# Planned order made binding: 21 stores and 64 loads of a 4096³ matmul with gelu wait for semaphores

## The chip, the cores and the metric

The kernel runs on one core of one Trainium2 chip. The metric is the device time in microseconds (us) of one execution; each kernel is run several times and the median is given. The core has five instruction streams that run beside each other: TensorE (PE, with its weight loads shown apart as PEld), VectorE (DVE), ScalarE (ACT), GpSimd (POOL) and SyncE (SP). In this kernel POOL and SP issue the transfers: POOL all loads, SP all stores.

## The reference

```python
def setup_inputs():
    m, k, n = 4096, 4096, 4096
    return {"a": np.random.randn(m, k).astype(np.float32),
            "b": np.random.randn(k, n).astype(np.float32)}

def reference(a, b):
    x = np.matmul(a, b)
    return 0.5 * x * (1 + np.tanh(np.sqrt(2 / np.pi) * (x + 0.044715 * x**3)))
```

One 4096×4096×4096 product and a gelu in its tanh form on every element; inputs and output are float32.

## The kernel before

**Products.** A and B are each cut into 2×2 quarters, named "11", "12", "21" and "22", and the product is formed with seven products P1 to P7 of sums and differences of quarters, in float16 with float32 sums (a Strassen scheme). The output is made in 16 groups: four row blocks `mb` of A times four column blocks `nb` of B. One group is a 512×512 block in each of the four output quarters. Group 0 (`first_group`) computes part of its work plainly and so can start before the sums exist; groups 1 to 3 use the seven products; groups 4 to 15 run in pairs (`late_pair`), in which some products are split a second time.

**Data.** A cell is a tile of 128×2048 float16 (512 KB); cells are named `bR`, `aD`, `aT` and `stage` after the pool they lie in. Raw rows of A and B come from DRAM through POOL (`stage<-in_a_dram`, `bR<-in_b_dram`), which turns float32 into float16 on the way. DVE transposes A (L752) and forms the sums and differences (L1039), TensorE multiplies (L822 in group 0 to 3, L2068 in the pairs). Ready sums of B are kept: SP stores them as units to DRAM (`k_unit<-bR`, `k_unit<-aD`, `k_unit<-stage`, from `store_unit`), and POOL fetches them in later groups (`bR<-k_unit`). SP also writes the output (`out_dram<-y`). All transfers are issued in one helper, so that all have the line L913.

**The squares.** Beside the product the kernel sums squares of A and B on ACT (L1437, L1459, L1504) to learn whether float16 sums are safe for these inputs; if they are not, a plain path runs. In two pairs `weigh_again` loads rows of A a second time for that, eight times four transfers of `bR<-in_a_dram`.

**What sets the order.** The program is recorded as a list of operations. `Plan.add` (L424) notes for each its engine, its duration by a table of costs, and which earlier operations it depends on, through the cells that it reads and writes. `Plan.schedule` simulates the engines with these costs, a table `AFTER` moves some operations by hand, and `Plan.emit` (L601) writes the operations out in the order of their planned starts. On the chip each engine takes its own instructions in that order. The waits between engines come from the framework, which sees the tiles that an instruction reads and writes.

**Gates.** Some transfers are recorded with `after=`: an earlier operation behind which they are planned although they share no data with it. It takes part in the simulated schedule and so in the order of the instructions, but the framework knows nothing of it, and the engine does not wait. One single pair of operations (`HOLD`, 1645 behind 1568) has had a real wait added. The transfers with gates are these:

- In `first_group`, `gate = load_a_("12", 1)[-1:]` (L2456) is a load of the second half of A's quarter "12", of the raw rows `stage<-in_a_dram`. Behind it are planned the units P7, lower half (L2460), and P5, upper half (L2471): two transfers each, the first four stores that SP issues.
- Later in `first_group`, `send(3, ...)` and `send(9, ...)` hold back twelve output blocks behind loads for group 1. `keep_t("P4", t1, ...)` (L2524) stores two transfers behind the last load of group 1's quarter "12" of B, and P5, lower half, and P6, upper half (L2525 and L2526) four behind the last load of quarter "22".
- In the pairs, the 32 transfers of `weigh_again` (L1453) and the 16 of `cast_unit` (L1693 and L2164, `k_unit<-in_b_dram`) stand behind the product operation nine back (`CAST_BACK`), and 16 transfers of `turn_quad` stand behind a fetch of product P1's units.

**Lanes.** Every transfer adds to one of eight semaphores of its queue when it has landed, in turn (`DMASW0` to `DMASW7` for POOL's, `DMAHW0` to `DMAHW7` for SP's). A wait on such a semaphore's value is a wait for one transfer's landing.

Of the kernel before, what the change touches and what calls it, by code (L numbers as in the profile page):

```python
# [80 lines left out]
def modes_of(**kw):  # L81
# [14 lines left out]
HOLD = {  # L96
    1645: 1568,
}
# [314 lines left out]


class Op:
    __slots__ = ("n", "eng", "dur", "fn", "deps", "succ", "key", "left", "ready", "need", "front", "start", "end", "size", "weight", "every", "frees")


class Plan:
# [4 lines left out]
    def add(self, eng, dur, fn, r=(), w=(), size=0, batch=None, after=(), slack=18.0, weight=1.0, every=None, lead=0.0):  # L424
        o = Op()
        o.every = dur if every is None else every
        o.weight, o.frees = weight, []
        o.n, o.eng, o.dur, o.fn, o.size = len(self.ops), eng, dur, fn, size
        deps = set(after)
        r, w = self.halves(r), self.halves(w)  # L430
        for tok in r:
            st = self.state.setdefault(tok, [[], [], None, ()])
            deps.update(st[0])
            st[1].append(o)
        for tok in w:
            st = self.state.setdefault(tok, [[], [], None, ()])
            if batch is not None and st[2] == batch and not [x for x in st[1] if x is not o]:
                deps.update(st[3])
                st[0].append(o)
                continue  # L440
            st[3] = set(st[0]) | {x for x in st[1] if x is not o}
            deps.update(st[3])
            st[0], st[1], st[2] = [o], [], batch
        deps.discard(o)
        o.deps, o.succ, o.key = deps, [], self.now + (slack if eng != "PE" else 0.0)
        for d in deps:
            d.succ.append(o)
        o.need = self.now + (max(slack, SLACK2) if eng != "PE" else 0.0)
        o.key, o.need = (x - EARLIER.get(o.n, 0.0) - lead for x in (o.key, o.need))
        o.left, o.ready = len(deps), 0.0  # L450
        self.ops.append(o)
        if eng == "PE":
            self.now += dur
        return o
# [145 lines left out]
    def emit(self):  # L600
        self.schedule()  # L601
        self.schedule(self.moved_order())
        done = {}
        for o in sorted(self.ops, key=lambda o: (o.start, o.n)):
            o.fn()
            done[o.n] = self.tc.nc.cur_bb.bb.instructions[-1]
            if o.n in HOLD:
                self.tc.add_manual_dep(
                    done[o.n], done[HOLD[o.n]].name,
                    mybir.DependencyInfo(mybir.DependencyClass.Sync, mybir.DependencyReason.DATA),  # L610
                    reason="later",
                )
# [2007 lines left out]
```

## Time and profile before

| | before |
|---|---|
| runs, us | 1467.91, 1457.4, 1468.47 (median 1467.91) |
| profiled execution, us | 1462.97 |
| its span, first to last instruction, us | 1461.3 |
| mean granted TensorE clock | 0.994 |
| busy: PE, DVE, ACT, POOL | 1424.8, 1225.1, 684.4, 506.6 us |
| moved by DMA | 389.36 MB, mean 266 GB/s |
| of it POOL's queue (q0, software) | 255.91 MB, 74.8% of 16 engines' span |
| of it SP's queue (q1, hardware) | 132.15 MB, 24.1% |

How to read it: a row of a timeline gives start, duration, engine, line, operation, `out<-in`, shapes and count, and in brackets the idle time of the engine just before and what ended it. The releaser in the brackets is inferred from semaphore events; where the engine it names had long been done, the wait was for another thing, often a transfer. A row of the waits gives the total idle time in us, how often, and the longest. A row of the table by windows gives the window, its length, the busy time of PE, PEld, DVE, ACT and POOL (with counts), the granted clock, the DMA share and GB/s. The DMA share is the sum of the time that packets took over that of 16 engines; it can be over 1 where packets of two queues overlap on an engine. "To landing" is the time from the issue of a transfer to its landing.

### The profile page before, as it was taken

What the parts mean: (1) busy time and instruction counts of PE and PEld (TensorE: products, weight loads), DVE (VectorE), ACT (ScalarE), POOL (GpSimd) and SP (SyncE); (2) the same over time, 40 slices, a digit from 0 to 9 for tenths busy, and PEclk for the clock granted to TensorE, in tenths of its full rate; (3) what the DMA queues carried; (4) which work ended last, traced back from release to release, by engine and by line L of the source; (5) the groups of instructions that cost most, each with busy time, mean ns of one, the idle gap of its engine ahead of it and who ended that gap; (6) DMA issues with size and microseconds to landing.
All of it is one profiled execution on the core that took longest, in us unless ns stands there. A gap on an engine that the chain in (4) does not pass through costs nothing.

```text
span 1461.3 us, 19125 instructions
## 1 busy us (share of the span) xinstructions
PE 1424.8 (98%) x6707; PEld 656.6 (45%) x6707; DVE 1225.1 (84%) x1319; ACT 684.4 (47%) x1376; POOL 506.6 (35%) x924
## 2 busy tenths in 40 slices
PE   8979999999999999999999999999999999999998
PEld 3434455465444444444444444444444444444443
DVE  2786797997878999978997989878998998867877
ACT  3505555439867322443645524353453734432133
POOL 7554236054125142324333352432323242231220
PEclk9989999999999999999999999999999999999999
DMA  9999999999999998989989999999898998895764
GB/s 173 211 208 263 301 278 227 372 240 262 325 288 227 314 231 212 329 279 263 296 315 290 305 198 296 304 256 308 250 337 241 308 238 262 264 295 213 267 230 182
DMA packets 216375, 389.36 MB, mean 266 GB/s; under 512 B 21456, under 2 KB 128464, under 8 KB 216272
## 3 DMA queue, kind: packets, MB, share of 16 engines
q0 software_dynamic: 159104, 255.91, 74.8%
q1 hardware_dynamic: 57168, 132.15, 24.1%
q8 instruction: 55, 0.90, 0.2%
q14 instruction: 48, 0.39, 0.1%
HBM read 356.52 MB, written 134.22 MB: 336 GB/s over the span
## 4 chain that ended last, share of the span: by engine, by line
PE 58%; DMA 14%; DVE 4%; issue 3%; POOL 1%; ACT 0%; SPq 0%; DVEq 0%; POOLq 0%; ACTq 0%
PE acc L2068 57%; DMA bR<-in_b_dram 5%; DMA bR<-in_a_dram 3%; DMA bR<-k_unit 3%; DVE bR L1039 2%; DMA stage<-k_unit 1%; PE acc L822 1%; POOL bR L913 1%; DMA k_unit<-bR 1%; DMA out_dram<-y 1%; DVE y L1397 1%; PE acc L1120 1%; DMA stage<-in_a_dram 1%; DVE y L1509 0%; DMA stage<-in_b_dram 0%
## 5 line engine op out<-in xcount | busy, mean ns | idle before, releaser
L2068 PE MATMUL acc<-bR 128*128 128x512 f16 x1344 | 300.2, 380 | 3.1 <-DVE bR L1039 2.9
L2068 PE MATMUL acc<-bR,aT 128*128 128x512 f16 x1280 | 284.2, 379 | 5.9 <-DVE bR L1039 5.0
L2068 PEld LDWEIGHTS <-bR 128*128 128x128 f16 x1824 | 178.5, 98 | 221.9 <-issue 5.9
L2068 PEld LDWEIGHTS <-aT 128*128 128x128 f16 x1664 | 162.6, 98 | 203.9 <-DMA bR<-in_b_dram 2.8
L913 POOL DMA_DIRECT2D bR<-in_b_dram x336 | 182.2, 545 | 188.1 <-DMA bR<-in_b_dram 31.4
L913 POOL DMA_DIRECT2D bR<-k_unit x210 | 114.0, 546 | 333.2 <-PE acc L2068 199.6
L1039 DVE TENSOR_TENSOR bR<-bR 128x4096 f16<-128x4096 f16 (+1 forms) x107 | 194.8, 1828 | 24.7 <-PE acc L2068 9.1
L2080 ACT COPY acc<-acc 128x512 f32<-128x512 f32 x168 | 95.9, 575 | 252.9 <-PE acc L2068 211.5
L1397 DVE TENSOR_TENSOR y<-acc,y 128x512 f32<-128x512 f32 x269 | 175.9, 685 | 24.4 <-PE acc L2068 21.9
L2068 PE MATMUL acc<-bR,aD 128*128 128x512 f16 x752 | 167.4, 379 | 1.4 <-DVE aD L1039 0.9
L2068 PEld LDWEIGHTS <-aD 128*128 128x128 f16 x1024 | 100.1, 98 | 122.8 <-DVE aD L1039 1.4
L1371 ACT ACTIVATE y<-y 128x512 f32<-128x512 f32 x174 | 105.6, 626 | 91.5 <-DVE y L1397 91.5
L822 PE MATMUL acc<-bR,aT 128*128 128x512 f16 x544 | 120.4, 379 | 2.1 <-DMA bR<-in_b_dram 1.0
L822 PEld LDWEIGHTS <-aT 128*128 128x128 f16 x768 | 75.0, 98 | 91.8 <-issue 3.0
L1504 ACT ACTIVATE y<-bR 128x1024 bf16<-128x1024 f16 x86 | 88.5, 1052 | 56.4 <-DVE y L1509 52.4
L2068 PE MATMUL acc<-stage,bR 128*128 128x512 f16 x480 | 108.0, 379 | 0.9 <-DVE bR L1039 0.9
L2077 ACT COPY y<-acc 128x512 f32<-128x512 f32 x114 | 65.3, 586 | 81.5 <-PE acc L2068 70.1
L822 PEld LDWEIGHTS <-aD 128*128 128x128 f16 x608 | 60.2, 99 | 87.5 <-DVE aD L1039 9.4
L913 POOL DMA_DIRECT2D bR<-in_a_dram x108 | 63.2, 590 | 95.7 <-ACT y L1437 46.4
L1509 DVE TENSOR_TENSOR y<-y 128x1024 bf16<-128x1024 bf16 x102 | 69.8, 686 | 23.1 <-ACT y L1504 21.6
L1402 DVE TENSOR_TENSOR acc<-acc,y 128x512 f32<-128x512 f32 x115 | 76.7, 693 | 13.8 <-ACT y L2077 13.7
L2068 PE MATMUL acc<-stage,aT 128*128 128x512 f16 x384 | 86.8, 379 | 0.4 <-DMA stage<-k_unit 0.4
(126 smaller groups left out, 1821.9 us busy)
## 6 DMA issues: line engine op xcount, KB each, us to landing
bR<-k_unit POOLq DMA_DIRECT2D x210, 512.0 KB, 7.5
out_dram<-y SPq DMA_DIRECT2D x194, 256.0 KB, 6.5
bR<-in_b_dram POOLq DMA_DIRECT2D x344, 128.0 KB, 6.4
k_unit<-bR SPq DMA_DIRECT2D x80, 512.0 KB, 6.9
stage<-k_unit POOLq DMA_DIRECT2D x74, 512.0 KB, 7.1
bR<-in_a_dram POOLq DMA_DIRECT2D x108, 256.0 KB, 8.6
k_unit<-stage SPq DMA_DIRECT2D x28, 512.0 KB, 7.5
out_dram<-bR SPq DMA_DIRECT2D x56, 256.0 KB, 6.2
```

The costliest lines, as they stand in the source:

```text
L822: nc.tensor.matmul(acc, sa[:, j // 2, i * P : (i + 1) * P, j % 2], sb[:, j, :], start=start and j == 0, stop=stop and j == 3, skip_group_c ...
L913: return plan.add(queue, COST[queue], lambda: eng.dma_start(out=dst, in_=src), r=r, w=w, size=MOVE[what] * SPREAD, weight=weight, **kw)
L1039: nc.vector.tensor_tensor(out=dst, in0=xa, in1=ya, op=ALU.add if op > 0 else ALU.subtract)
L1120: nc.tensor.matmul(PS[s][i][:, :] if wide else PS[s][i][:, w * HC : (w + 1) * HC], sa[:, j // 2, r * P : (r + 1) * P, j % 2], rhs(j, wide) ...
L1371: act("gelu", lambda: nc.scalar.activation(t, t, ACT.Gelu_apprx_tanh), [("f", f)], [("f", f)])
L1397: dve("add", lambda: nc.vector.tensor_tensor(out=sm(g), in0=bank(s, i), in1=sm(f), op=ALU.add), [("f", f)], [("f", g), ("p", s, i)])
L1402: dve("add", lambda: nc.vector.tensor_tensor(out=bank(s, i), in0=bank(s, i), in1=sm(f), op=ALU.add), [("f", f)], [("p", s, i)])
L1504: act("square", lambda t=t, src=src: nc.scalar.activation(t, src, ACT.Square), [c(cx)], [("f", f)], slack=60.0, lead=lead)
L1509: dve("add16", lambda t=t, u=u: nc.vector.tensor_tensor(out=u, in0=u, in1=t, op=ALU.add), [("f", f)], [("f", e)], slack=60.0, lead=lead)
L2068: nc.tensor.matmul(bank(w, i), sa[:, jx // 2, r * P : (r + 1) * P, jx % 2], bv[:, jx, :], start=p in "17" and jx == 0, stop=jx == NJ - 1, ...
L2077: act("copy", lambda: nc.scalar.copy(out=sm(f), in_=bank(w, i)), [("p", w, i)], [("f", f)])
L2080: act("copy", lambda: nc.scalar.copy(out=bank(*dst), in_=bank(*x)), [("p", *x)], [("p", *dst)])
```

## The change

Each transfer that is recorded with `after=` now keeps those of its `after` operations that are not dependencies through data, as `gates`. `emit` gives each gate to the framework as a real dependency, as it did for `HOLD` alone, so that the issuing engine waits on a semaphore until the gate's operation is done: until it has landed, where it is a transfer. The schedule is computed from the same dependencies as before. 21 stores on SP and 64 loads on POOL get a gate.

```diff
-    __slots__ = (..., "every", "frees")
+    __slots__ = (..., "every", "frees", "gates")
...
-        deps = set(after)
+        deps = set()
         r, w = self.halves(r), self.halves(w)
...
         deps.discard(o)
+        o.gates = [x for x in after if size and x not in deps]
+        deps.update(after)
         o.deps, o.succ, o.key = deps, [], self.now + (slack if eng != "PE" else 0.0)
...
             done[o.n] = self.tc.nc.cur_bb.bb.instructions[-1]
-            if o.n in HOLD:
+            for n in [x.n for x in o.gates] + [HOLD[k] for k in [o.n] if k in HOLD]:
                 self.tc.add_manual_dep(
-                    done[o.n], done[HOLD[o.n]].name,
+                    done[o.n], done[n].name,
                     mybir.DependencyInfo(mybir.DependencyClass.Sync, mybir.DependencyReason.DATA),
                     reason="later",
                 )
```

The rows of all five engines stand in the same order as before; only waits differ. Lines of the changed file from L447 on carry a number higher by two (L913 becomes L915).

SP's queue, its first five transfers, before; `k_unit` is a unit in DRAM, `aD` and `bR` are cells, and the names in brackets are the semaphores that the instruction waits for:

```order
L913 DMA k_unit_218<-aD_82 128x2048 [waits DMASW2_49,DMASW1_49,DMASW3_49,DMASW0_49,DVE_49]
L913 DMA k_unit_217<-bR_73 128x2048 [waits DMASW6_49,DMASW7_49,DMASW5_49,DMASW4_49]
L913 DMA k_unit_218<-aD_82 128x2048
L913 DMA k_unit_217<-bR_73 128x2048
L913 DMA k_unit_217<-bR_74 128x2048 [waits DMASW3_49,DMASW4_49,DMASW2_49,DMASW6_49,DMASW0_49,DVE_49]
```

The same rows now:

```order
L915 DMA k_unit_218<-aD_82 128x2048 [waits DMASW2_49,DMASW1_49,DMASW3_49,DMASW0_49,DVE_49]
L915 DMA k_unit_217<-bR_73 128x2048 [waits DMASW6_49,DMASW7_49,DMASW5_49,DMASW4_49]
L915 DMA k_unit_218<-aD_82 128x2048
L915 DMA k_unit_217<-bR_73 128x2048
L915 DMA k_unit_217<-bR_74 128x2048 [waits DMASW4_49,DMASW3_49,DMASW6_49,DMASW2_49,DVE_49]
```

No row has moved and the names on the first row are the same. The value that it waits for on `DMASW0` is another: it was the count after eight transfers on that lane, and is now the count after twelve, the twelfth being the gate, a load `stage<-in_a_dram`. That is why the fifth row needs no wait on that lane any more.

SP's queue further on, rows 28 to 32 (end of group 0, start of group 1), before:

```order
L913 DMA k_unit_222<-stage_86 128x2048 [waits DMAHW3_49,DVE_49]
L913 DMA k_unit_220<-aD_82 128x2048 [waits DMAHW4_49]
L913 DMA k_unit_220<-aD_82 128x2048 [waits DMAHW5_49]
L913 DMA k_unit_222<-stage_86 128x2048 [waits DMAHW6_49,DVE_49]
L913 DMA k_unit_222<-stage_87 128x2048 [waits DMAHW7_49,DVE_49]
```

and now:

```order
L915 DMA k_unit_222<-stage_86 128x2048 [waits DMAHW3_49,DVE_49]
L915 DMA k_unit_220<-aD_82 128x2048 [waits DMAHW4_49,DMASW1_49]
L915 DMA k_unit_220<-aD_82 128x2048 [waits DMAHW5_49]
L915 DMA k_unit_222<-stage_86 128x2048 [waits DMAHW6_49,DVE_49]
L915 DMA k_unit_222<-stage_87 128x2048 [waits DMAHW7_49,DVE_49]
```

The second row has got a wait on `DMASW1`, the landing of a POOL load `bR<-in_b_dram`; the rows behind it are issued after it.

POOL's queue in the pair of groups 8 and 9, before (`bR<-in_a_dram` are two of the rows of A that are loaded again for their squares, `k_unit` are fetches):

```order
L913 DMA bR<-k_unit 128x2048 [waits DMASW6_49,PE_49]
L913 DMA bR<-in_a_dram 32x8x512 [waits DMASW7_49]
L913 DMA bR<-in_a_dram 32x8x512 [waits DMASW0_49]
L913 DMA stage<-k_unit 128x2048 [waits DMAHW7_49,DMASW1_49]
L913 DMA bR<-k_unit 128x2048 [waits DMASW2_49,PE_49]
```

and now:

```order
L915 DMA bR<-k_unit 128x2048 [waits DMASW6_49,PE_49]
L915 DMA bR<-in_a_dram 32x8x512 [waits DMASW7_49,PE_49]
L915 DMA bR<-in_a_dram 32x8x512 [waits DMASW0_49]
L915 DMA stage<-k_unit 128x2048 [waits DMAHW7_49,DMASW1_49]
L915 DMA bR<-k_unit 128x2048 [waits DMASW2_49]
```

The first load of A waits for a product on TensorE, and the fetch two rows behind the second load has lost its own wait for TensorE, since that one came earlier.

More of the change, by code (lines that the diff above doesn't have):

```diff
@@ L415 @@
 class Op:
-    __slots__ = ("n", "eng", "dur", "fn", "deps", "succ", "key", "left", "ready", "need", "front", "start", "end", "size", "weight", "every", "frees")
+    __slots__ = ("n", "eng", "dur", "fn", "deps", "succ", "key", "left", "ready", "need", "front", "start", "end", "size", "weight", "every", "frees", "gates")
 class Plan:
```

## Prediction

> **What bounds the kernel now.** The page first. TensorE is busy nearly throughout, so time can be won only where it stands, or where its clock is halved.
>
> ```profile
> span 1461.3 us, 19125 instructions
> PE 1424.8 (98%) x6707; PEld 656.6 (45%) x6707; DVE 1225.1 (84%) x1319; ACT 684.4 (47%) x1376; POOL 506.6 (35%) x924
> ```
>
> Then the waits of TensorE: the longest single one, and by its side the total of the pairs' commonest one.
>
> ```profile
> PE acc L2068 <- DVE bR L1039: 8.8, 6, 2.6
> PE acc L822 <- DVE aD L1039: 8.4, 1, 8.4
> ```
>
> The timeline of TensorE shows where the long pauses lie: 8.40 us ahead of 86.69, and three more rows on which terms rest, at 152 to 191 us.
>
> ```profile
> 86.69 9.16 PE L822 MATMUL acc<-aD 128*128 128x512 f16 x32 [8.40 <-DVE aD L1039]
> ...
> 152.26 7.07 PE L822 MATMUL acc<-bR,aT 128*128 128x512 f16 x32 [1.02 <-DMA bR<-in_b_dram]
> 159.16 7.07 PE L822 MATMUL acc<-stage,aD 128*128 128x512 f16 x32
> 168.29 22.57 PE L822 MATMUL acc<-stage,aD 128*128 128x512 f16 x96 [2.06 <-DVE stage L1039]
> ```
>
> The timeline of VectorE tells what the 8.40 us are. The sum at 85.41 that TensorE waits for follows two transposes of `stage` at 83.01, and VectorE itself had stood 5.94 us for a load of A.
>
> ```profile
> 77.67 1.25 DVE L752 STREAM_TRANSPOSE aT<-aD 128x1024 uint32<-128x1024 uint32 x1 [5.94 <-DMA aD<-in_a_dram]
> 83.01 2.37 DVE L752 STREAM_TRANSPOSE aT<-stage 128x1024 uint32<-128x1024 uint32 x2
> 85.41 1.23 DVE L1039 TENSOR_TENSOR aD<-aT 128x2048 f16<-128x2048 f16 x1
> ```
>
> The loads that it stood for were issued from 62 to 68 us, and the view of that tile on POOL gives their time from issue to landing; four loads of the same kind issued from 84 to 87 us took 5.3 to 8.5 us:
>
> ```profile
> DMA to landing us min/median/max: 15.7/15.8/16.6
> ...
> DMA to landing us min/median/max: 5.3/7.8/8.5
> ```
>
> SP's timeline says what stood beside the slow ones: its first four stores, the first and the last of which begin these two rows (the second row has two later ones in it), with the landing of all four, and the share of the 16 DMA engines that SP's queue had from 62 to 84 us.
>
> ```profile
> 62.80 0.34 SPq L913 DMA_DIRECT2D k_unit<-aD  x1
> 65.00 35.26 SPq L913 DMA_DIRECT2D k_unit<-bR  x3
> ...
> DMA to landing us min/median/max: 7.3/9.0/10.4
> ...
> q1 hardware_dynamic: 576, 2.10, 25.4%
> ```
>
> **The change part by part.** *First stores.* They now wait for the gate, a load issued first of the four here; with the 5.3 us it landed at 89.4. Behind the waiting instruction the other three stores queue, and nothing else before SP's next row at 98 us, which waits for VectorE.
>
> ```profile
> 84.13 2.55 POOL L913 DMA_DIRECT2D stage<-in_a_dram  x4 [0.42 <-issue]
> 97.71 2.20 POOL L913 DMA_DIRECT2D bR<-in_b_dram  x4 [0.41 <-issue]
> ```
>
> (a) Without the stores the loads of 62 to 84 us have 25.4% × 22 = 5.6 us more of the DMA engines. I take it that they land 5.6 us earlier. VectorE's 5.94 us of idle time allow that, and the pause shrinks from 8.40 to 2.8 us. Bounds: nothing, if the loads are limited by their own queue; 5.6 us. I leave the half clock behind this pause as it is, since the 2.06 us pause, below, halved it too.
>
> (b) The stores' 5.6 us of DMA work aren't gone, only later, and TensorE's pause at 152.26 is for a load. What is issued earlier before it can land earlier there only as far as the DMA engines had time to spare. The table by windows (PE, PEld, DVE, ACT, POOL, granted clock, DMA share, GB/s) shows how much:
>
> ```profile
> 70.00:80.00 10.00, 7.35 (x34) 3.03 (x32) 4.06 (x6) 1.55 (x2) 2.72 (x5) 1.00 1.31 259
> 80.00:90.00 10.00, 3.31 (x8) 1.19 (x9) 9.96 (x12) 0.00 (x0) 5.99 (x11) 0.53 1.30 192
> 90.00:100.00 10.00, 10.00 (x45) 4.42 (x44) 10.00 (x13) 0.00 (x0) 6.29 (x12) 0.95 1.24 185
> 100.00:110.00 10.00, 10.00 (x47) 4.49 (x46) 9.44 (x12) 3.17 (x5) 3.79 (x7) 1.00 1.14 241
> 110.00:120.00 10.00, 10.00 (x49) 4.51 (x47) 9.97 (x13) 0.68 (x2) 7.57 (x14) 1.00 1.03 139
> 170.00:172.00 2.00, 2.00 (x6) 0.76 (x5) 1.90 (x3) 0.88 (x1) 0.00 (x0) 0.50 1.18 298
> ```
>
> A full DMA shows 1.28 (mean of the first three). The two windows from 100 to 120 us fall short by 11% and 20%, which is 1.1 + 2.0 = 3.1 us. So I keep 3.1 of the 5.6 us, an estimate, and give back 2.5. Bounds: 0 and 5.6.
>
> *Later stores of group 0.* The other gate that binds is that of the second of these rows; its stores queue ahead of a row that VectorE releases at 168 us anyway.
>
> ```profile
> 156.87 0.97 SPq L913 DMA_DIRECT2D k_unit<-aD  x2
> 157.94 10.64 SPq L913 DMA_DIRECT2D k_unit<-stage  x2
> ...
> DMA to landing us min/median/max: 7.8/9.6/10.7
> ...
> q1 hardware_dynamic: 575, 2.10, 49.3%
> ```
>
> The last row is SP's queue from 156.4 to 168 us; the one above it the landing of three of its four stores. The gate is the second load in this row of POOL's timeline, issued at 157.57. From issue to landing it took 9.3 us (the second row here), to 166.9, and VectorE's sum at 167.01 starts as it lands; the TensorE named in its bracket had long been done.
>
> ```profile
> 156.93 4.40 POOL L913 DMA_DIRECT2D bR<-in_b_dram  x7 [0.15 <-issue]
> ...
> DMA to landing us min/median/max: 9.3/9.3/9.3
> ...
> 167.01 1.23 DVE L1039 TENSOR_TENSOR stage<-bR,stage 128x2048 f16<-128x2048 f16 x1 [4.44 <-PE acc L822]
> ...
> 173.22 1.22 DVE L1039 TENSOR_TENSOR aD<-aD,aT 128x2048 f16<-128x2048 f16 x1
> ```
>
> (c) The load had four stores beside it and will have one. Three quarters of 49.3% × 11.6 us = 5.7 us is 4.3 us, more than the 2.06 us that TensorE waits, so that pause goes, with 2.2 us in hand. Behind it 96 products took 22.57 us, where 32 start every 6.90 us (152.26 to 159.16): 3 × 6.90 + 0.17 = 20.87, so the half clock cost 1.70. Sum −3.76. Bounds: 0 and −3.76.
>
> The granted clock is 0.50 from 170 to 172 us, behind a pause of 2.06 us. [...] The measured 0.50 decides here.
>
> (d) The three stores are issued as the gate lands: 166.9 − 4.3 − 3.1 = 159.5. They read cells that VectorE writes later, at 173.22 in this trace and, 6.9 us sooner (3.1 + 3.76), at 166.3. The quickest store is out at 159.5 + 7.8 = 167.3, the slowest at 170.2: up to 0.9 or 3.9 us late, of which TensorE may see all or nothing. I take 0.9, as it is the first store's cell.
>
> *Loads in the pairs.* (e) Three holds are longer than 5 us; these are two of them. Each row has its product on TensorE and POOL's next row behind the loads:
>
> ```profile
> 891.96 0.61 POOL L913 DMA_DIRECT2D bR<-in_a_dram  x1
> 897.88 7.07 PE L2068 MATMUL acc<-bR,aT 128*128 128x512 f16 x32
> 908.37 0.57 POOL L913 DMA_DIRECT2D stage<-k_unit  x1 [14.81 <-DMA k_unit<-stage]
> ...
> 1234.79 0.61 POOL L913 DMA_DIRECT2D bR<-in_a_dram  x1
> 1241.04 3.62 PE L2068 MATMUL acc<-stage,aD 128*128 128x512 f16 x16
> 1248.59 0.55 POOL L913 DMA_DIRECT2D bR<-k_unit  x1 [13.18 <-PE acc L2068]
> ```
>
> The load at 891.96 must now wait for the product's end at 904.95, 13.0 us later; behind it stand another load of A and then a fetch that stood 14.81 us anyway, until 908.37. The load of 1234.79 waits for 1244.66, 9.9 us, ahead of a row at 1248.59 that waited for TensorE. In both the idle time ends 3.4 and 3.9 us after the gate, which hides the hold; without that cover each would push the fetches behind it. I take 0; bound +3. Gates already met on SP (the output blocks, the stores of P5 and P6) cost nothing.
>
> Sum: −3.1 − 3.76 + 0.9 + 0 = −6.0 us; by the page's rule on the clock, −4.3.
>
> **Base.** The profiled execution took 1462.97 us (span 1461.3 and 1.7 around it), 4.9 less than the median of the runs, 1467.91; they lie from 1457.4 to 1468.47. I count from the middle of the two, 1465.4, as I can't tell which the next median is nearer to. The forecast is 1465.4 − 6.0 = 1459.4 us.
>
> **Rivals.**
>
> *The first stores plug the loads (slower).* Rows 97.71 and on refill cells that the four stores read, so POOL waits for their landing. From the gate to the last landing they need 65.00 + 10.4 − 62.80 = 12.6 us, taking the slowest landing for the last store. With the gate at 89.4 − 5.6 = 83.8 they are done at 96.4, in time by 1.3. If the gate opens after 85.1, the point from which this decides, POOL is held: at 89.4, unmoved, the stores land at 102.0, POOL loses 4.3 us and TensorE's pause for a load at 152.26 grows by as much, and is then long enough to halve the clock (1.7). With the second pause gone: 4.3 + 1.7 − 3.76 = +2.2, 1467.6. For it: the gate's load stands behind eight loads that each waited for a landing. Against: those land earlier.
>
> *The early gain stays whole.* If loads to 152 us are not short of DMA time, −5.6 − 3.76 + 0.9 = −8.5: 1456.9. For it: GB/s falls to 139 at 110 to 120 us. Against: the 1.02 us pause for a load.
>
> *All of it is given back,* and only the second pause goes: −3.76, 1461.6. For it: the same pause.
>
> *The half clock at 170 us has another cause* and stays: −3.1 − 2.06 + 0.9 = −4.3, 1461.1. Against: 0.50 right behind the pause. [...]
>
> *The gate on the first store does nothing.* Only (c) is left, 1461.6. In the order the names of its semaphores are as they were. Against: its value has grown, as the fifth row dropped a wait on the same lane.
>
> *The held loads drain POOL's queue.* If what waits behind the three long holds is late by a whole load each, 3 × 5.3 = 15.9, less 6.0: +9.9, 1475.3. Against: the 14.81 and 13.18 us in which POOL stood with TensorE busy.
>
> **How the numbers follow.** Chances: forecast 0.43, plug 0.22, early gain whole 0.14, all given back 0.08, other cause of the clock 0.05, gate does nothing 0.03, drained queue 0.05. The forecast's own range, with the spread of the runs (1457.4 − 6.0, 1468.47 − 6.0), is 1451 to 1463; the plug reaches 1470, the whole early gain 1450. Only the drained queue and the rims lie outside 1450 to 1470. A measurement of this kernel can tell about 1%, 14.7 us: faster is under 1453.2, slower above 1482.6. The first takes the lower rim of the forecast or of the whole gain, 0.12; the second a drained queue worse than worked out, 0.04; within 1% is 0.84.
>
> **What would show it.** Right: the loads `stage<-in_a_dram` of 62 to 68 us land in about 10 us; the 8.40 us pause is near 2.8; SP's first store stands at 84 us; no pause ahead of TensorE's 96 products and no half clock there; the pairs' waits are as before. Wrong: the first pause unchanged (a), a pause over 2 us near 152 (plug), the second pause there (c), new pauses of TensorE near 905 or 1245 us (e).

## The result, and the profile after

The changed kernel takes 1452.25 us (median of 13 runs, 1444.55 to 1458.13), the kernel before 1462.42 us in as many runs (1457.4 to 1470.85). The ratio is 0.9925, 95% interval 0.9901 to 0.9949: 11.0 us less, between 7.5 and 14.5. Timed a second time, with other runs of both, the ratio was 0.9945 (0.992 to 0.9969), 8.0 us less, between 4.5 and 11.7. The forecast was 1459.4 us with a range of 1450 to 1470, and 6.0 us less. The sign is right and the gain larger: 6.0 lies below the first interval and inside the second. The profiled execution took 1454.51 us, against 1462.97. Three single runs in what follows were slow, at a lower clock (1501.56 us of e4, 1496.28 of e5, 1481.07 of the kernel before beside e1 to e4); the ratios leave them out, the medians do not.

The timeline of TensorE after the change, at the places shown of before:

```profile
81.04 8.45 PE L824 MATMUL acc<-aD 128*128 128x512 f16 x32 [2.85 <-DVE aD L1041]
...
98.80 5.34 PE L824 MATMUL acc<-bR,aT 128*128 128x512 f16 x24 [0.68 <-ACT acc L2483]
...
146.81 7.07 PE L824 MATMUL acc<-bR,aT 128*128 128x512 f16 x32 [1.11 <-DMA bR<-in_b_dram]
153.72 27.79 PE L824 MATMUL acc<-stage,aD 128*128 128x512 f16 x128
181.34 17.43 PE L824 MATMUL acc<-bR,aT 128*128 128x512 f16 x80
```

The first pause is 2.85 us instead of 8.40. The same product that waited for a load until 152.26 starts at 146.81, 5.45 us sooner. The second pause is gone, and with it the half clock: 128 products run through in one row of 27.79 us. The row that starts at 181.34 serves as a mark, as the kernel before starts it here (timeline of TensorE, before):

```profile
190.69 17.43 PE L822 MATMUL acc<-bR,aT 128*128 128x512 f16 x80
```

So at that point the changed kernel is 9.35 us ahead; its whole span is 8.4 us shorter (1461.3 and 1452.9). In this pair of traces everything that it gains is gained in the first eighth.

SP's and VectorE's timelines, the landing of the raw loads of A into `stage` issued from 62 to 68 us, and the share of the DMA engines that POOL's queue had from 62 to 84 us (SP's queue has no line there any more), all of the changed kernel:

```profile
83.86 0.34 SPq L915 DMA_DIRECT2D k_unit<-aD  x1
...
72.02 1.25 DVE L754 STREAM_TRANSPOSE aT<-aD 128x1024 uint32<-128x1024 uint32 x1 [0.39 <-DMA aD<-in_a_dram]
...
77.35 2.37 DVE L754 STREAM_TRANSPOSE aT<-stage 128x1024 uint32<-128x1024 uint32 x2
...
79.76 1.23 DVE L1041 TENSOR_TENSOR aD<-aT 128x2048 f16<-128x2048 f16 x1
...
DMA to landing us min/median/max: 10.2/10.7/10.8
...
q0 software_dynamic: 7434, 4.17, 136.5%
```

The first store went from 62.80 to 83.86 us. The loads take 10.7 us to land where they took 15.8, POOL's queue has 136.5% where it had 101.7%, VectorE stands 0.39 us for the load of A where it stood 5.94, and the sum that ends the pause starts at 79.76 instead of 85.41: 5.65 us.

The loads that VectorE itself stood for go into `aD`; POOL issued them just ahead of those of `stage`, at 59.7 to 61.6 us before and 60.1 to 62.0 us after. Their landing, before and then after:

```profile
DMA to landing us min/median/max: 12.9/15.0/15.9
...
DMA to landing us min/median/max: 7.8/8.9/9.9
```

The slowest of them lands 6.0 us sooner. The same shows in every run below: the loads into `stage` of 62 to 68 us take 15.8 to 16.5 us by the median in the four kernels whose first stores don't wait (before, e2, e4, e12) and 10.4 to 11.8 us in the ten others.

The wait list of TensorE in the pairs has one new pause of over 2 us, at 717 us (2.57 us, in the second row here); where it comes from is taken up below.

```profile
PE acc L2070 <- DVE bR L1041: 6.9, 5, 1.9
PE acc L2070 <- DMA bR<-k_unit: 3.2, 2, 2.6
PE acc L824 <- DVE aD L1041: 2.8, 1, 2.8
```

### The profile page after: what moved, and what is told of

It reads as the page before. It is cut to its first block, busy times and chain, and to the rows that moved or that the text cites. A ratio compares the mean times of both kernels' runs of the same rounds, so it can differ in the third digit from the quotient of the medians.

```text
span 1452.9 us, 19128 instructions
## 1 busy us (share of the span) xinstructions
PE 1422.1 (98%) x6707; PEld 656.0 (45%) x6707; DVE 1224.8 (84%) x1319; ACT 684.2 (47%) x1376; POOL 506.4 (35%) x924
## 4 chain that ended last, share of the span: by engine, by line
PE 72%; DMA 17%; POOL 4%; issue 3%; DVE 3%; ACT 1%; SPq 0%; DVEq 0%; POOLq 0%; ACTq 0%
PE acc L2070 61%; PE acc L824 10%; DMA bR<-in_b_dram 5%; DMA bR<-in_a_dram 4%; DMA bR<-k_unit 3%; DMA stage<-in_a_dram 3%; POOL bR L915 3%; PE acc L1122 2%; DVE bR L1041 1%; DMA seen_d<-seen 1%; DMA stage<-in_b_dram 1%; DMA aD<-in_a_dram 1%; POOL stage L915 1%; DVE y L1399 0%; DVE y L1511 0%
## 5 line engine op out<-in xcount | busy, mean ns | idle before, releaser
L915 POOL DMA_DIRECT2D bR<-in_b_dram x336 | 182.1, 545 | 177.5 <-DMA bR<-in_b_dram 27.4
L915 POOL DMA_DIRECT2D bR<-k_unit x210 | 114.1, 546 | 306.0 <-PE acc L2070 197.5
L915 POOL DMA_DIRECT2D bR<-in_a_dram x108 | 63.1, 589 | 134.6 <-PE acc L2070 45.4
L824 PEld LDWEIGHTS <-aD 128*128 128x128 f16 x608 | 59.7, 98 | 78.8 <-issue 4.9
```

What stands on the lines that cost most here:

```text
L824: nc.tensor.matmul(acc, sa[:, j // 2, i * P : (i + 1) * P, j % 2], sb[:, j, :], start=start and j == 0, stop=stop and j == 3, skip_group_c ...
L915: return plan.add(queue, COST[queue], lambda: eng.dma_start(out=dst, in_=src), r=r, w=w, size=MOVE[what] * SPREAD, weight=weight, **kw)
```

## The experiments

The theory: two gates make the gain, that of SP's first four stores 5.5 us and that of P4's upper half 3.8 us; the loads held in the pairs are hidden. The rivals: the first gate alone does it all; the held loads take part.

All kernels are the changed one with the set of gates, or one gate, altered. Each was timed in 12 runs beside 34 or 35 runs of the kernel before on the same chip. The mark in the table is the start of the row of 80 products that stands at 190.69 us before and at 181.34 us after; it leaves out what the pairs do later.

| run | gates | mark, us | median, us | before, us | ratio (95%) |
|---|---|---|---|---|---|
| before | none | 190.69 | | | |
| after | all | 181.34 | 1452.25 | 1462.42 | 0.9925 (0.9901 to 0.9949) |
| e1 | stores | 182.94 | 1456.19 | 1461.53 | 0.9965 (0.994 to 0.999) |
| e2 | loads | 189.98 | 1460.65 | 1461.53 | 0.9995 (0.9973 to 1.0018) |
| e3 | first four stores | 183.27 | 1458.11 | 1461.53 | 0.9976 (0.9951 to 1.0002) |
| e4 | P4's two stores | 184.86 | 1458.07 | 1461.53 | 0.9985 (0.9957 to 1.0013) |
| e5 | all, first later | 184.17 | 1457.22 | 1462.63 | 0.995 (0.9921 to 0.998) |
| e6 | all, first earlier | 181.76 | 1453.35 | 1462.63 | 0.9933 (0.9909 to 0.9958) |
| e7 | all and one more | 180.57 | 1453.09 | 1462.63 | 0.9935 (0.9912 to 0.9959) |
| e8 | all and two more | 181.88 | 1453.42 | 1462.63 | 0.9931 (0.9905 to 0.9958) |
| e9 | all | 179.18 | 1452.89 | 1462.42 | 0.9945 (0.992 to 0.9969) |
| e10 | stores | 180.83 | 1452.38 | 1462.42 | 0.9947 (0.9922 to 0.9972) |
| e11 | first four and P4's two | 179.11 | 1455.49 | 1462.42 | 0.9954 (0.9925 to 0.9984) |
| e12 | loads | 186.57 | 1458.4 | 1462.42 | 0.9984 (0.9962 to 1.0005) |

**The first gate alone (e3).**

```diff
-        o.gates = [x for x in after if size and x not in deps]
+        o.gates = [x for x in after if size and x not in deps and x.n == 173]
```

Operation 173 is the load that the first four stores wait for.

> Only the first four stores of SP wait for their gate, the load of the raw rows of A. Theory (two gates, two gains): the first pause falls from 8.4 to 2.8 us and this is kept at 152 us of the old trace, 5.5 us; the pause of 2.1 us ahead of the 96 products and the half clock behind it stay: 5 to 6 us under before. Rival (the first gate does all: with the loads 5.5 us earlier the second pause goes by itself): 9 us under before, no second pause.

TensorE's timeline in this run:

```profile
147.18 7.07 PE L824 MATMUL acc<-bR,aT 128*128 128x512 f16 x32 [2.01 <-DMA bR<-in_b_dram]
...
162.56 20.88 PE L824 MATMUL acc<-stage,aD 128*128 128x512 f16 x96 [1.40 <-DVE stage L1041]
183.27 17.00 PE L824 MATMUL acc<-bR,aT 128*128 128x512 f16 x78
```

The first pause was 2.9 us, and at the load before 147.18 TensorE was 5.1 us ahead of the old trace: the gain is kept. The second pause is still there, 1.40 us. That is against the rival in which the first gate does it all. But the half clock behind the second pause did not come (96 products in 20.88 us, which is the time that the prediction worked out for full speed), so this run gains 7.4 us at the mark and not 5 to 6. By the times it is 3.5 us under before, with an interval that holds 1.

**The gate of P4's upper half alone (e4).** The same line with `x.n == 389`.

> Only the two stores of P4's upper half wait for their gate, a load of B for group 1. Theory: the first pause stays 8.4 us; the second pause (2.1 us) and the half clock behind it (1.7 us) go: 3.8 us under before. Rival (the second pause goes only because of the first gate): no change, the second pause stays. Rival (the stores held there are late for the cells that VectorE writes next): the gain is smaller by up to 0.9 us.

The waits of TensorE and its timeline:

```profile
PE acc L824 <- DVE aD L1041: 7.9, 2, 7.6
...
157.23 27.79 PE L824 MATMUL acc<-stage,aD 128*128 128x512 f16 x128
184.86 15.49 PE L824 MATMUL acc<-bR,aT 128*128 128x512 f16 x71
```

The first pause stays (7.6 us; 8.4 in the trace of before), the second and its half clock are gone: 128 products in 27.79 us. At the mark 5.8 us are gained, of which 0.8 are the shorter first pause in this one trace, and 1.0 is the wait for a load that before had at 152 us and this trace does not have. That the second pause goes without the first gate is as the theory has it. The time, 2.2 us under before, has an interval that holds 1: the times alone show neither single gate, the pauses and the marks do. No pause shows a late store.

**Stores alone and loads alone (e1, e2, e10, e12), and the two gates (e11).** The gates kept are those with `eng == "SP"`, with `eng == "POOL"`, and with `x.n in (173, 389)`.

> Only the 21 stores wait for their gates; the 64 loads of the pairs are planned as before. Theory (both gains are made by stores in group 0, the held loads are hidden): the same as the whole change, 8 to 10 us under before, TensorE 9.3 us ahead at the trace's 190 us. Rival (the held loads of the pairs help, by leaving the DMA engines to the fetches): part of the gain is missing, 3 us or more. Second rival (the held loads cost something): 1 to 3 us better than the whole change, without new pauses of TensorE behind 700 us.

> Only the 64 loads of the pairs wait for their gates; all stores are issued as before. Theory: 0, within 1.5 us of before, both pauses in group 0 (8.4 and 2.1 us) as before. Rival (the held loads help): 3 us or more under before. Rival (they drain the queue): up to 16 us over.

> The change as it is, timed beside the three others on the same chip. Theory (the gain is the stores'; the runs with the stores alone came out smaller by chance, as single times spread by 5 us to either side): 8 to 11 us under before and within 3 us of the run with the stores alone. Rival (the held loads add something that they show only together with the stores): 8 to 11 us under before and 4 us or more under the stores alone.

> Only the 21 stores wait for their gates, once more, beside the whole change. Theory: within 3 us of the whole change. Rival: 5 us under before, 4 us or more over the whole change.

> Only two gates are left: that of the first four stores and that of P4's upper half; the 15 other stores and all loads are planned as before. Theory (the other stores' gates were met before the store came up): the same as all 21 stores, within 3 us. Rival (the gates of the output blocks or of P5 and P6 hold something): 3 us or more away from all 21 stores.

> Only the 64 loads of the pairs wait for their gates, once more. Theory: within 2 us of before. Rival (the held loads help by themselves): 3 us or more under before.

At first the stores alone came out 5.3 us under before, where the whole change, timed apart, had come out 10.2 under. That could be the loads' part, so all were timed side by side: the whole change 9.5 us under before by the medians, the stores alone 10.0, the two gates 6.9, the loads alone 4.0. The whole and the stores are equal there, which speaks against a part of the loads that shows only with the stores. The loads alone missed their expectation by the medians, 4.0 us under before where at most 2 were expected; by the ratio it is 2.3. Both of their intervals hold 1, and the times alone don't exclude a gain of 4 to 6 us by them. The traces speak against it: all held loads lie behind the mark, and from the mark to the end it takes 1270.6 us in the mean of the six traces with held loads (after, e2, e5, e6, e9, e12) and 1269.1 us in the six without (before, e1, e3, e4, e10, e11). The 15 other stores are eleven output blocks (not twelve, as said ahead) and four units. The two gates came out 3.1 us over all stores by the medians, at the edge of the 3 us expected, and 1.0 us over by the ratios, with the earliest mark of all; so the 15 show no effect that these runs tell apart.

The marks say the same for the stores, with less noise. With both gates they stand at 181.34, 182.94, 179.18, 180.83 and 179.11 us (after, e1, e9, e10, e11), 180.7 in the mean; with none of the stores' gates at 190.69, 189.98 and 186.57 us (before, e2, e12), 189.1 in the mean. That is 8.4 us for the two gates, 5.8 for the first alone (e3) and 4.2 for P4's alone (e4), each of the last two from one trace. Marks lie up to 3.8 us apart among the kernels with both gates and up to 4.1 us among those with none, so the two single sizes are good to some us only, and need not add up to 8.4.

POOL's timeline of the changed kernel shows why the held loads of the pairs cost nothing:

```profile
900.26 1.19 POOL L915 DMA_DIRECT2D bR<-in_a_dram  x2 [13.28 <-PE acc L2070]
901.43 0.57 POOL L915 DMA_DIRECT2D stage<-k_unit  x1
...
1239.12 0.60 POOL L915 DMA_DIRECT2D bR<-in_a_dram  x1 [10.16 <-PE acc L2070]
1242.75 0.55 POOL L915 DMA_DIRECT2D bR<-k_unit  x1 [3.03 <-PE acc L2070]
```

POOL stood 14.81 us behind the loads before; it now stands 13.28 us ahead of them, and the fetch follows at once. It is the same idle time, on the other side of the load. The fetch of 1242.75 again waits for TensorE, behind the held load.

**The gate five loads later (e5).** The load is operation 318, in place of 173:

```diff
-            for n in [x.n for x in o.gates] + ...
+            for n in [318 if x.n == 173 else x.n for x in o.gates] + ...
```

> The whole change, but the first four stores wait for a load five places further on (one of B into the raw cells), which landed at 92.2 us in the trace of the changed kernel, 8.4 us after the gate. Theory of the plug: the stores land at about 105 us instead of 96.8, POOL's load of 97.4 us, which refills their cells, is held some 7.5 us, and TensorE's pause for a load at 146.8 us grows by as much, with a half clock behind it: 7 to 9 us over the changed kernel. Rival (POOL catches up, because the DMA engines have time to spare behind 100 us): the pause at 146.8 us grows by 3 us at most, and the kernel stays within 3 us of the changed one.

POOL's and TensorE's timelines in this run:

```profile
99.52 2.14 POOL L915 DMA_DIRECT2D bR<-in_b_dram  x4 [10.16 <-DMA k_unit<-bR]
...
147.96 8.75 PE L824 MATMUL acc<-bR,aT 128*128 128x512 f16 x32 [2.70 <-DMA bR<-in_b_dram]
```

The gate opened at 87.9 us, not at 92.2; that the five loads, without stores beside them, landed sooner too would explain it, but is not shown here. POOL stood 10.16 us for the stores' landing, but its load came only 2.2 us later than after the change (POOL's timeline there):

```profile
97.36 0.54 POOL L915 DMA_DIRECT2D bR<-in_b_dram  x1 [2.42 <-DMA k_unit<-bR]
```

TensorE's pause for the load grew from 1.11 to 2.70 us, and the 32 products behind it ran in 8.75 us instead of 7.07. At the mark that is 2.8 us lost, by the ratios about 2.5 (7.3 us under before, where the three others timed beside it are 9.5 to 10.1 under, with intervals that overlap). So the wait exists, and TensorE's pause grew as the rival had it, by 1.6 us and not by 7.5. By these figures it costs some 2 to 4 us, which is not shown beyond doubt: the pause at this load is up to 2.04 us long in traces with the gate in its place (e10).

**The gate nine loads earlier (e6).** Operation 123 in place of 173.

> The whole change, but the first four stores wait for the last load of A that VectorE's transposes at 77.4 us need, which landed at 77.2 us, 6.6 us before the gate. Theory (only the loads up to that one matter for the first pause): the first pause stays 2.8 us, the stores land near 90 us, no wait of POOL for a store's landing near 97 us, TensorE's pause at 146.8 us at most as long: the same as the changed kernel or up to 1 us better. Rival (the loads of B behind it are then late, since the stores stand beside them): a new pause of TensorE between 90 and 120 us of 1 to 5 us.

The stores went at 77.54 us. The first pause was 3.09 us, the mark 181.76 us, the median 9.3 us under before: the same as the changed kernel. No pause came up between 90 and 120 us beyond 0.5 us. Only the loads up to that one matter for the first pause here, and between 77 and 84 us the place of the gate makes no difference that these runs show.

**The same kind of gate in another place (e7, e8).** At 383 us of the changed kernel six stores stand beside four loads of raw A, and TensorE pauses at 398.76 for a sum behind them.

```diff
-            for n in [x.n for x in o.gates] + [HOLD[k] for k in [o.n] if k in HOLD]:
+            for n in [x.n for x in o.gates] + [t[k] for t in (HOLD, {1408: 1389}) for k in [o.n] if k in t]:
```

In e8 the table is `{1408: 1389, 1193: 1374}`.

> The whole change and one gate more, of the same kind in another place: the stores from 383.5 us on wait for the last of four loads of raw A issued at 378.2 us, which took 15.7 us to land with six stores beside them. If the mechanism carries over (stores beside a load that VectorE waits for lengthen it): the load lands 4 to 7 us sooner, TensorE's pause of 2.7 us at 398.8 us goes, 2 to 3 us under the changed kernel at that point. Rival (the pause only moves, to 374 us, or the held stores keep cells from VectorE): no gain at 410 us.

> As the run with one gate more, and a second: the stores from 371.9 us on wait for the last of four loads of raw A issued at 364.5 us, which landed at 380.7 us. If the mechanism carries over, the pause of 1.8 to 4.3 us near 374 us that most traces show is shorter by what the four stores from 371.9 us took, up to 2 us, as eight stores are under way before that and are not held. Rival (output blocks held there come free later and stop ScalarE and VectorE): a new pause of TensorE near 380 us, 2 us or more over the run with one gate.

The landing of the four loads issued from 378 us on, and the pause, in the changed kernel:

```profile
DMA to landing us min/median/max: 8.0/10.9/15.7
...
398.76 3.61 PE L824 MATMUL acc<-bR,aD 128*128 128x512 f16 x16 [2.74 <-DVE bR L1041]
```

and with the gate, where the pause at that place is gone (e7):

```profile
DMA to landing us min/median/max: 8.0/9.4/10.4
...
442.85 5.12 PE L2070 MATMUL acc<-bR,aT 128*128 128x512 f16 x16 [2.71 <-DVE bR L1041]
```

The slowest load lands 5.3 us sooner and the pause is gone, as expected. But this pair of traces doesn't show that the gate did it: in e9, which is the changed kernel with no further gate, the same four loads land within 7.3 us and the pause at 399 us is missing too, with one of 1.73 us at 364 us in its place. And 44 us on, TensorE of e7 pauses 2.71 us where it paused 0.64 us, its 16 products then taking 5.12 us instead of 3.63, and the median is that of the changed kernel. In e8 the pause at 399 is gone too, and 2.90 us stand at 445.91. Whether the gate's second part shortens the pause near 374 us can't be told: the changed kernel's trace has none there. So it stays open whether the mechanism carries over; a gain does not show, and in both runs a longer pause stands at 443 to 446 us. No version here beats the changed kernel by more than these times tell apart.

## Why the prediction was right, and where it was off

**(a) The first pause.** Right in size: 5.6 us forecast, 5.55 measured (8.40 to 2.85), by the cause that was named; over the traces the pause is 7.6 to 8.4 us without the gate and 1.6 to 3.1 us with it. The loads that VectorE stood for were those of `aD`, issued just ahead of the loads named in the prediction; both kinds landed 5 to 6 us sooner. That the size came out so near is in part luck: it was SP's share of the DMA engines, 25.4% of 22 us, taken as time that the loads get back. But POOL's queue rose by more than that share, from 101.7% to 136.5%, so it passes 1 with no packets of SP's queue beside it, and is not time that is handed over. The gate opened at 83.8 us as worked out (SP's row at 83.86). The half clock behind the pause was left in the sum as it was; it was in part kept, 32 products in 8.45 us where they had taken 9.16 (granted clock 0.50 from 81 to 83 us, before 0.50 from 86 to 90), and in six of ten traces with the gate it is gone (7.1 us).

**(b) What is kept of it.** This is the step that was mis-sized. 3.1 of 5.6 us were to be kept, by the time that the DMA engines had to spare; 5.45 us were kept at the load of 146.81 (5.1 in e3). Over all traces, the row behind the 32 products that wait there (153.72 in the changed kernel) starts at 153.4 us in the mean with the gate in its place and at 158.4 without: 5.0 us are kept. The rival "the early gain stays whole" had it, at 0.14. The error lay in taking the DMA share for a measure of what is to spare. The share of 1.28 at 70 to 100 us went with 185 to 259 GB/s, that of 1.14 at 100 to 110 us with 241 GB/s; it isn't a fill level. A row that tells more is on POOL, before:

```profile
127.91 2.14 POOL L913 DMA_DIRECT2D bR<-in_b_dram  x4 [9.34 <-DVE y L1397]
```

and after:

```profile
121.89 2.68 POOL L915 DMA_DIRECT2D bR<-in_b_dram  x5 [6.29 <-DVE bR L1041]
```

POOL, on its way to the load for which TensorE waits at 152 us, stood over 9 us at 128 us until other engines had come so far; after the change it went on 6.0 us sooner, and at 135.28 instead of 140.30 behind a second wait for ScalarE. All traces agree: this row starts at 119.3 to 123.7 us with the first gate and at 127.3 to 129.0 without. Whose work ended the wait is not settled: the profile names VectorE in these two traces, the landing of a store in others (e3, e10).

**(c) The second pause.** Right: it is gone, with the half clock, in all traces that have the gate of P4's upper half (after, e1, e4 to e11), and stays in those that don't (2.06 us in before, 1.40 in e3, 1.85 in e2, 1.83 in e12). The load on which it hangs landed 6.2 us after its issue instead of 9.3, 3.1 us sooner and not 4.3; the 2.06 us needed were covered, with 1.0 in hand and not 2.2. SP's row, with the two stores held until then, and the landing of that load, both of the changed kernel:

```profile
158.54 0.80 SPq L915 DMA_DIRECT2D k_unit<-aD  x2
...
DMA to landing us min/median/max: 6.2/6.2/6.2
```

The price of the half clock, 1.70 us, is real only in the trace of before: in e2, e3 and e12 the 96 products take 20.88 us behind the pause, which is full speed. So −3.76 is what this gate was worth in one of four traces; in the three others it would have been 1.4 to 1.9 us. The −4.3 that stands beside the sum rests on a rule on the clock that no run shows; what the runs showed is a granted clock of 0.50 from 170 to 172 us behind the pause of 2.06 us (before), and full speed behind the pauses of 1.40 to 1.85 us (e3, e12, e2).

**(d) The held stores late for VectorE.** 0.9 us were put in, and TensorE saw nothing: no pause of it stands near there. VectorE waits 0.24 us for a store's landing at 168.83 us.

**(e) The held loads.** Right, 0, by the cover that was named, as far as POOL's rows and the stretch behind the mark tell.

**The plug.** The gate opened before 85.1, so it did not decide. Forecast was a last landing at 96.4 us; it was 96.8, and POOL did stand 2.42 us for a store (row shown above). In e6, where the stores go 6.3 us earlier and POOL stands for none of them, the mark is no earlier, so this cost nothing that shows. Moved by 4.1 us (e5), POOL's wait came up as told, 10.16 us, at a price of some 2 to 4 us instead of 6.0.

The terms as seen in these two traces, 5.45 and 3.8, make 9.3 us, which is the 9.35 of the two at the mark; the mean over the traces is 8.4. The forecast's 6.0 lacks 2.4 us of (b) and the 0.9 of (d). The rest of the distance between 1459.4 and 1452.25 is mostly the base: 1465.4 us was taken from four runs, 13 runs have a median of 1462.42.

**What spreads the times.** From the mark to the end of the span it took 1270.6 us before (1461.3 − 190.69), 1271.6 after, 1266.6 in e3, 1263.1 in e7, 1275.5 in e5, 1262.5 in e12. These 13 us go with no edit, e12 and e2 (1269.0) being the same kernel. They go for the most part with TensorE's pauses behind the mark, which add up to 8.4 and 8.7 us in the two shortest (e7, e12) and to 16.0 to 18.0 us in the three longest (e5, e6, e8). These pauses, of up to 4 us, come at other places in each execution: the 2.57 us at 717 us of the changed kernel are one of them, since they are missing in e9, which is the same kernel, and in e5, e6 and e7. A single trace's end time says nothing on a change of this size; a mark close behind it says more, to within some 4 us.

## What to carry to other kernels

Where a pause of the bound engine goes back to a load, look at which transfers without a due time stand beside it on the other queue: here stores that nobody waited for, issued as soon as their data was there, made loads that VectorE and behind it TensorE stood for take 15.0 us by the median instead of 8.9. The planned order didn't hold them: SP, with nothing else to do, issued the first at 62.80 us, 21 us before it did with a semaphore on the load's landing. Whether an earlier load is passed on was better read from what the loading queue itself waits for further on (9.34 us at 128 us here) than from the DMA share, and how far the hold may go is bounded by the first load that needs the stores' landing (in e5 POOL stood 10.16 us for it).

## What the runs showed that was not expected

**In these traces the half clock doesn't go by the length of the pause alone.** In e1 a pause of 3.08 us is followed by full speed, and a pause of 2.03 us, 18 us later, by a lower clock:

```profile
81.80 7.10 PE L824 MATMUL acc<-aD 128*128 128x512 f16 x32 [3.08 <-DVE aD L1041]
...
99.56 7.03 PE L824 MATMUL acc<-bR,aT 128*128 128x512 f16 x24 [2.03 <-ACT acc L2483]
...
82.00:86.00 4.00, 4.00 (x20) 1.75 (x19) 4.00 (x6) 0.00 (x0) 2.53 (x5) 1.00 1.39 180
99.50:103.00 3.50, 3.44 (x10) 1.30 (x10) 3.40 (x4) 2.04 (x4) 1.52 (x3) 0.62 1.16 260
```

The last two rows are the table by windows, with the granted clock third from the end: 1.00 behind the longer pause, 0.62 behind the shorter. The 24 products of the second row took 7.03 us; in e9 the same 24 took 5.34 us behind a pause of the same length:

```profile
97.45 5.34 PE L824 MATMUL acc<-bR,aT 128*128 128x512 f16 x24 [2.03 <-ACT acc L2483]
```

So length alone doesn't decide in these traces: pauses of 2.06 (before, granted clock 0.50 from 170 to 172 us), 2.03 (e1, 0.62) and 2.70 us (e5, 32 products in 8.75 us instead of 7.07) were followed by slower products, those of 3.08 (e1) and 2.03 us (e9) were not. What else decides they don't show.

**A pause took the place of part of the first one.** In all traces with the first gate TensorE waits near 98 us for ScalarE's copy `acc<-acc`, 0.4 to 2.0 us, which the trace of before doesn't have. It goes with the clock and not with the gate: where the 32 products behind the first pause run at full speed (7.1 us; granted clock 1.00 in e1) it is 2.03 us, where they take 8.4 to 8.8 us (0.57 from 80 to 84 us after the change) it is 0.3 to 0.7 us, in e12 too, which has no first gate, and where they take over 9 us (0.50 in before) it is missing. From the first product behind the pause to the 24 products behind this wait it is 17.8 to 17.9 us in all ten traces with the gate, at either clock. So what a full clock wins there is waited for here, and leaving the half clock out of (a) did no harm. It cost nothing that the mark shows beyond the spread: e9 and e11 have 2.03 us there and the earliest marks of all.
